# A two-layer hybrid trunk on one core: linear-attention heads with buffers of their own and half their products on GpSimd, a low-rank gate block with stacked weights, shift tiles in groups of four

## The chip, the cores and the metric

The kernel runs on one core of a Trainium2 chip. The metric is the device time of one execution in microseconds (us); a time of a kernel is the median of several runs. The profile is one further execution, recorded by the hardware profiler.

## The reference

One inference step of a two-layer trunk over 128 context tokens and 512 latent tokens (640 columns in the kernel, `T`), width 2048. Every layer is an adaptively modulated RMSNorm, one wide input projection, two mixer branches side by side, a SiLU gate path, one output projection and a gated residual. The change lies in layer 0: its modulation, and its gated linear attention (4 heads, key width 128, value width 256, forward and backward scans, decays from a projection of rank 16 per direction).

```
shift, scale, gate = split(silu(cond) @ ada_w[l] + ada_b[l], 3)       # cond: one row for context, one for latents
h = rms_norm(x, norm_g[l]) * (1 + scale) + shift

# layer 0 (even): all columns of one projection
qa, ka, va, qb, kb, vb, rb, gp = split_cols(h @ w_in, EVEN_SPLITS)    # rb: 2 * 16 columns
ya = window_sink_attention(...)  or  ctx_attention(...)
logit = einsum('btdr,drk->btdk', rb, wg) + bg                         # low-rank gate
g = log_sigmoid(logit) / 16                                           # per direction d and head
for each chunk of tokens:                                             # gla_scan, forward and backward
    bcum = cumsum(g);  qi = q*exp(bcum);  ki = k*exp(-bcum);  ks = k*exp(blast - bcum)
    o = tril(qi @ ki.T) @ v + qi @ S
    S = exp(blast) * S + ks.T @ v
yb = rms_norm(o_f + flip(o_b), gnorm)
y = concat(ya, yb) * silu(gp);   x = x + gate * (y @ w_out[0])
# layer 1 (odd): neighbourhood attention || chunked spatial gating, same frame
```

Everything is float32.

## The kernel before

**Layout.** Tokens lie along the free dimension, features along the partitions. The modulated input stands in SBUF split in two float32r halves, `acth` (rounded) and `actl` (rest), 16 k-tiles of 128 features each with 2 + 640 columns: the first two columns carry the shift of the modulation, so that each product also gives the shift's contribution. A *block* (`chunk` in the code) is 128 output columns of a weight matrix. Its weights come by DMA into `wraw`, ScalarE writes the rounded half `whi`, GpSimd the rest `wlo = wraw - whi`, four k-tiles (512 columns) at a time; `whi` and `wlo` hold 2560 columns, so five such groups. TensorE then runs three products for each k-tile and each half of the tokens: `whi*acth`, `whi*actl`, `wlo*acth`, which makes 96 matmuls of 320 or 322 columns a block (`mm_k`, recorded under line 393). All of the later blocks of the network use this scheme, many of them in pairs with one recursion of Strassen's method.

**Order.** Nothing is scheduled by the compiler. The Python code emits the instructions in one pass and keeps a model clock for each engine (`Pace`). Blocks are emitted one after the other on TensorE; between their matmuls `tick` advances generator tasks (attention heads, linear heads, normalisation) whose inputs the model holds to be ready, pumps weight splits (`wpump`) and, when VectorE is ahead, a low-priority task that computes the modulation vectors of later stages. A task that needs another's result waits for a flag (`wait`); a block's evacuation that needs one calls `need`, which lets the model clock run. So a change of one cost, buffer or flag moves many instructions around it.

**Start (`start`).** Layer 0's scale and half of its shift are computed on TensorE: 24 tiles of 128 modulation features, 1 MB each, as two loads of 512 KB into a ring of six places (`Y`, `more`). A tile takes 16 matmuls `bank<-Y,cond` with 32 output rows and 128 columns (line 1360), a copy of the result to SBUF on ScalarE (`adas<-bank`), and a product with `sel` (in the tile `small`) that puts it into two columns. The other eight shift features come from `shifts`: 32 loads of 256 KB (`raw<-ada_s`), each multiplied with a row of the condition (`crow_s`, in PSUM and in `mixrow`) on VectorE or on GpSimd and summed into `sh`. At its end `sh` goes into the first two columns of `acth` and `actl` (lines 1082 and 1083) and is transposed on TensorE (`bank<-ident,sh`). Meanwhile the first six blocks (`FIRST`, without shift columns) run in windows of k-tiles as their inputs arrive. All large loads are issued by SyncE (SP) in the order written.

**Linear heads.** The first block with shift columns is `w_rb`, the 32 low-rank columns; the kernel repeats them three times to 96 rows, since the next product wants them as hi, hi and lo. Then for each head come the blocks of k, q and two of v, and two tasks: `gla_elem` makes the decays and the products `Qp`, `KS`, `QI`, `KI` (all 128x640) for both directions, `gla_pe` does the head's matmuls, fills `O` and normalises it. One set of buffers serves all heads: `O` is `Y[:, 4:6]`, the place of `QI` and `KI`; the normalisation shares the ring `gt` with the elementwise task; there is one `k`. So the elementwise task of a head begins with

```
if h:
    yield from self.wait(f"gla_done{h - 1}")
```

and the evacuations of its k and q blocks wait for the elementwise task of the head before (`gla_elem`). After head 3 follow two gate blocks, then attention, whose heads alternate with further gate blocks.

## Time and profile before

| | before |
|---|---|
| three runs, us | 2122.69, 2121.43, 2122.52; median 2122.52 |
| the profiled execution, us | 2118.93 |
| its span, us | 2117.1 |
| mean granted TensorE clock | 0.994 |
| busy: PE, PEld | 2058.0 us (97%), 2003.7 us (95%) |
| busy: DVE, ACT, POOL | 1320.0, 1071.2, 1285.1 us (62%, 51%, 61%) |
| DMA | 341 MB, 161 GB/s on the mean; over 350 GB/s in the first two of 40 slices |

PE is TensorE's matmuls, PEld its weight loads, DVE VectorE, ACT ScalarE, POOL GpSimd, SP SyncE. A row of a list of groups reads: line, engine, operation, output<-inputs, shapes, count | busy us, mean ns of one | idle us of the engine just before these instructions, and what ended it. A float32 matmul (the 32-row ones, the products with `ones`, `sel` or a head's tiles) leaves two records, a float32r one leaves one. Line 213 is the helper through which all instructions of DVE, ACT and POOL go, line 427 that of the DMAs on SP, so groups are told apart by their tiles.

### The profile page before, as it was taken

The page shows a single profiled execution, that of the slowest core. Times are in us where ns is not written, and L with a number is a line of the kernel's source. Part 1 is how long each engine was busy: PE and PEld are TensorE (multiplying, and loading weights), DVE is VectorE, ACT ScalarE, POOL GpSimd, SP SyncE. Part 2 cuts the span into 40 slices and gives each one's busy share as a digit, 9 for nine tenths or more (in the row PEclk, how much of TensorE's full clock was granted, in tenths as well). Part 3 has the DMA queues.
Part 4 walks back from the last instruction along what each step waited for, and adds up shares of the span by engine and source line. Part 5 has one row for each costly group of instructions (what it writes and reads, how often), then busy time and mean ns, then how long its engine had stood idle before and what let it go on. Part 6 is the DMA issues. An engine that isn't in the chain of part 4 may idle for free. (4 is left out here: it accounts for less than half of the span.)

```text
span 2117.1 us, 40263 instructions
## 1 busy us (share of the span) xinstructions
PE 2058.0 (97%) x14345; PEld 2003.7 (95%) x14345; DVE 1320.0 (62%) x3063; ACT 1071.2 (51%) x2471; POOL 1285.1 (61%) x1082
## 2 busy tenths in 40 slices
PE   7999999999999999999999999999999999999996
PEld 6899999999999999999999999999999999999995
DVE  4856686666556554988666878777454444465335
ACT  5645565454666665543564444444444544454433
POOL 4756564445545544888565656655555577668873
PEclk9999999999999999999999999999999999999998
DMA  9966343336464544576643455444322344354437
GB/s 363 398 226 189 121 158 107 111 119 197 130 206 150 150 136 145 187 229 219 213 130 105 136 160 159 143 139 149 94 81 90 108 139 130 124 202 132 128 95 248
DMA packets 193401, 341.23 MB, mean 161 GB/s; under 512 B 20944, under 2 KB 70192, under 8 KB 193200
## 3 DMA queue, kind: packets, MB, share of 16 engines
q1 hardware_dynamic: 191728, 337.10, 49.4%
q8 instruction: 112, 1.84, 0.4%
q10 hardware_dynamic: 1472, 1.56, 0.2%
q14 instruction: 89, 0.73, 0.1%
HBM read 304.08 MB, written 31.88 MB: 159 GB/s over the span
## 5 line engine op out<-in xcount | busy, mean ns | idle before, releaser
L393 PE MATMUL bank<-acth,whi 128*128 128x320 f32 (+2 forms) x3320 | 1021.5, 318 | 10.6 <-ACT bc L213 2.8
L393 PE MATMUL bank<-actl,whi 128*128 128x320 f32 (+2 forms) x3320 | 994.7, 310 | 3.7 <-DMA actl<-bl_dram 2.1
L393 PE MATMUL bank<-acth,wlo 128*128 128x320 f32 (+2 forms) x3320 | 994.5, 311 | 3.5 <-POOL wlo L213 3.5
L213 POOL TENSOR_TENSOR wlo<-wraw,whi 128x512 fp32r<-128x512 f32 (+1 forms) x452 | 573.6, 1281 | 412.1 <-ACT whi L213 329.8
L393 PEld LDWEIGHTS bank<-acth,whi 128*128 128x128 f32 (+1 forms) x3320 | 617.6, 189 | 20.9 <-ACT bc L213 3.9
L393 PEld LDWEIGHTS bank<-actl,whi 128*128 128x128 f32 (+1 forms) x3320 | 617.4, 189 | 6.9 <-DMA actl<-bl_dram 3.3
L393 PEld LDWEIGHTS bank<-acth,wlo 128*128 128x128 f32 (+1 forms) x3320 | 617.5, 189 | 5.1 <-POOL wlo L213 5.1
L213 POOL TENSOR_TENSOR wlo<-rs,whi 128x384 fp32r<-128x384 f32 x370 | 408.1, 1123 | 183.2 <-ACT whi L213 143.6
L213 ACT ACTIVATE whi<-wraw 128x512 fp32r<-128x512 f32 (+1 forms) x460 | 262.9, 588 | 93.2 <-PE bank L393 60.7
L393 PE MATMUL bank<-eh,wlo 128*128 128x322 f32 (+1 forms) x666 | 207.2, 311 | 2.7 <-POOL wlo L213 2.7
L393 PE MATMUL bank<-eh,whi 128*128 128x322 f32 (+1 forms) x666 | 209.3, 314 | 0.0
L393 PE MATMUL bank<-el,whi 128*128 128x322 f32 (+1 forms) x666 | 206.9, 311 | 0.0
L213 ACT ACTIVATE whi<-rs 128x384 fp32r<-128x384 f32 x370 | 182.0, 514 | 48.5 <-PE bank L393 41.7
L213 DVE TENSOR_TENSOR wraw<-rs 128x768 f32<-128x768 f32 x74 | 98.8, 1335 | 124.7 <-POOL wlo L213 69.9
L213 DVE CUSTOM_DVE_ANT_0 adas<-adas,bank,partg 128x256 bf16<-128x256 f32 (+1 forms) x290 | 156.2, 539 | 12.6 <-DMA adas<-ada_g 5.3
L213 POOL TENSOR_TENSOR prod<-adas,mixrow 128x512 f32<-128x512 f32 x85 | 111.5, 1321 | 70.4 <-ACT prod L213 48.5
L213 ACT ACTIVATE arena<-arena,bc 128x512 f32<-128x512 f32 (+4 forms) x211 | 106.4, 527 | 79.8 <-DVE arena L213 77.0
L393 PEld LDWEIGHTS bank<-eh,wlo 128*128 128x128 f32 x666 | 125.5, 189 | 3.9 <-POOL wlo L213 3.7
L393 PEld LDWEIGHTS bank<-eh,whi 128*128 128x128 f32 x666 | 125.7, 189 | 0.1
L393 PEld LDWEIGHTS bank<-el,whi 128*128 128x128 f32 x666 | 125.8, 189 | 0.0
L213 DVE CUSTOM_DVE_ANT_0 adas<-adas,bank,part 128x512 bf16<-128x512 f32 x151 | 112.4, 744 | 9.8 <-DMA adas<-ada 6.8
L213 ACT ACTIVATE arena<-Y 128x320 f32<-128x320 f32 (+1 forms) x76 | 38.9, 512 | 152.1 <-DVE Y L213 125.9
(218 smaller groups left out, 2480.1 us busy)
## 6 DMA issues: line engine op xcount, KB each, us to landing
wraw<-w_even SPq DMA_DIRECT2D x176, 256.0 KB, 3.4
adas<-ada_g SPq DMA_DIRECT2D x128, 256.0 KB, 3.7
adas<-ada SPq DMA_DIRECT2D x128, 256.0 KB, 3.8
rs<-w_odd SPq DMA_DIRECT2D x50, 384.0 KB, 3.3
wraw<-w_odd SPq DMA_DIRECT2D x74, 256.0 KB, 3.5
wraw<-w_out SPq DMA_DIRECT2D x64, 256.0 KB, 3.9
rs<-w_odd SPq DMA_DIRECT2D x50, 256.0 KB, 3.8
Y<-ada SPq DMA_DIRECT2D x24, 512.0 KB, 7.3
```

Source lines behind the costliest of these rows:

```text
L213: return f(*args, **kw)
L393: self.nc.tensor.matmul(out, lhsT, rhs, start=start, stop=stop, **kw)
```

## The change

1. **Low-rank block.** The weights keep 32 columns; `whi` now holds hi and lo side by side (64 columns), and two products per k-tile and half, with `acth` and with `actl`, make 64 matmuls with 64 output rows (`quad`). Both token halves are copied to SBUF, and a float32 product with a 0/1 matrix `rep` adds hi and lo rows and repeats the sum to 96 rows.
2. **Start.** The eight shift tiles go in two groups of four: 16 matmuls of 512 columns, loads waited for and refilled four at a time, one copy of 512 columns, four products with `sel`. The copy of the very first tile moves from ACT to DVE. `cT` is loaded by ACT's queue instead of SP's; the constants needed later (`late`, 176 KB, and the sinks) are loaded after the start. `mixrow` has one place instead of two.
3. **Linear heads.** `O` of heads 0 to 2 lies in `YB`, the normalisation has a ring `nt` of its own, `k` has two places, `Qp` and `QI` are made on GpSimd. The elementwise task waits for the one before it; `gla_free` of the head before (its last read of `Qp`) is awaited ahead of the first `Qp`, and its `gla_done` ahead of writing `O`. Gate block 14, which lies in the place of `O`, needs `gla_done2`.
4. **Attention.** Gate block 2 moves from before head 7's query block to behind it.

```
+GROUPS = (*((f, 1) for f in range(KT)), *((f, 4) for f in range(KT, KT + BOTH, 4)))
...
-        nc.sync.dma_start(self.cT, d["cT"])
+        nc.scalar.dma_start(self.cT, d["cT"])
...
-        self.mixrow = [self.t(yb, [128, PIECE], "mixrow", bufs=2) for _ in range(2)]
+        self.mixrow = [self.t(yb, [128, PIECE], "mixrow")] * 2
...
-        if m < M:
-            raw = raw[:, :, None, :].to_broadcast([128, n, M // m, m])
-            hi, lo = (x.rearrange("p a (b c) -> p a b c", c=m) for x in hl)
+        if key[0] in self.stacked:
+            hl = hi
+            hi, lo = hl[:, :, :m], hl[:, :, m:]
         nc.scalar.activation(hi, raw, AF.Copy)
...
+    def quad(self, c, parts):
...
+        for half, p in enumerate(banks):
+            cs = self.cols(half, shift)
+            n = cs.stop - cs.start
+            for u in units:
+                w = self.wget(u)
+                for j in range(4):
+                    for i, x in enumerate((self.ah, self.al)):
+                        k = u[1] + j
+                        self.mm(p[:M, :n], w[:, j, :], x[:, k, cs], start=k == i == 0, stop=k == KT - 1 and i == 1)
+                    if j % 2:
+                        self.tick()
+            self.nc.scalar.activation(parts[half][:M, :n], p[:M, :n], AF.Copy)
+            self.drop(p)
+        for u in units:
+            self.wdone(u)
+
+        def work():
+            for half, x in enumerate(parts):
...
+                yield from self.until(x)
+                yield from self.bank()
+                p = self.sm()
+                self.mm(p[:96, : x.shape[1]], self.rep[:M, :], x)
+                evac(*((None, p) if half else (p, None)))
+                yield
...
             def tiles():
-                for i in range(KT + BOTH):
-                    ws = [ring[(2 * i + q) % NR].rearrange("p (a b) -> p a b", b=128) for q in range(2)]
-                    yield from self.until(*ws)
...
+                for i, n in GROUPS:
+                    m = 8 // n
+                    for b in range(0, 2 * n, 4):
+                        e = min(b + 4, 2 * n)
+                        ws = [ring[(at + q) % NR].rearrange("p (a b) -> p a b", b=128 * n) for q in range(e - b)]
+                        yield from self.until(*ws)
+                        self.now += 0.2
+                        for k in range(m * b, m * e):
+                            g = 32 * (k % 4)
+                            o, c, w = pm[g : g + 32, 0 : 128 * n], cond[:, k, :], ws[k // m - b][:, k % m, :]
+                            self.pe(0.0575 * n, o, c, w)
+                            nc.tensor.matmul(o, c, w, start=k < 4, stop=k >= KT - 4)
...
+                        for q in range(e - b):
+                            load(at + q + NR)
...
+                    r = rows.next()[:, : 128 * n]
+                    if i == 0:
+                        nc.vector.tensor_copy(r, pm[:, : 128 * n])
+                    else:
+                        nc.scalar.activation(r, pm[:, : 128 * n], AF.Copy)
...
+            nc.sync.dma_start(self.late, d["late"])
+            nc.sync.dma_start(self.sink, d["attn_sink"].partition_broadcast(128))
             while self.tasks or self.low:
...
         if h:
-            yield from self.wait(f"gla_done{h - 1}")
+            yield from self.wait(f"gla_elem{h - 1}")
...
-            nc.vector.tensor_tensor(L["Qp"][dr], q, e3, ALU.mult)
+            if dr and h:
+                yield from self.wait(f"gla_free{h - 1}")
+            nc.gpsimd.tensor_tensor(L["Qp"][dr], q, e3, ALU.mult)
...
-            nc.vector.tensor_tensor(L["QI"][dr], q, e4, ALU.mult)
+            nc.gpsimd.tensor_tensor(L["QI"][dr], q, e4, ALU.mult)
...
+        if h:
+            yield from self.wait(f"gla_done{h - 1}")
         yield from self.until(At, Sb)
         outs((0, 1), (None, S))
...
-        sq, sq2 = L["gt"].next(), L["gt"].next()
+        sq, sq2 = L["nt"].next(), L["nt"].next()
...
+                self.need("gla_done2")
                 ev(pa, pb)
...
-            L["O"] = Y[:, 4:6, :]
+            L["O"] = (*(self.YB[:, KT - NY - 2 :, :],) * 3, Y[:, 4:6, :])
...
-            add(wE[16 + h], 128, True, None, lazy("k", pre=p))
+            add(wE[16 + h], 128, True, None, lazy("k", pre=(f"gla_elem{h - 2}",) if h > 1 else (), then=keep))
...
-                if kv and h != 5:
+                if h in (4, 6):
...
-        for i in (3, 4, 5):
+        for i in (2, 3, 4, 5):
             gate_chunk(wE[28 + i], self.yt(i), (f"ya{i}",), "gx")
```

TensorE at the end of the low-rank block, before: the last two k-tiles of `w_rb` in bank 68, then the first k-tile of head 0's keys in bank 69.

```order
L393 MATMUL bank_68<-acth,whi 96x320
L393 MATMUL bank_68<-actl,whi 96x320
L393 MATMUL bank_68<-acth,wlo 96x320
L393 MATMUL bank_69<-acth,whi 128x322
L393 MATMUL bank_69<-actl,whi 128x322
L393 MATMUL bank_69<-acth,wlo 128x322
```

The same place in the change; `late` is the tile that holds `rep`, `arena` the copy of the block's result.

```order
L398 MATMUL bank_68<-acth,whi 64x320
L398 MATMUL bank_68<-actl,whi 64x320
L398 MATMUL bank_69<-acth,whi 128x322
L398 MATMUL bank_69<-actl,whi 128x322
L398 MATMUL bank_69<-acth,wlo 128x322
L398 MATMUL bank_69<-acth,whi 128x322
L398 MATMUL bank_69<-actl,whi 128x322
L398 MATMUL bank_69<-acth,wlo 128x322
L398 MATMUL bank_71<-arena_1538,late 96x322
```

The third product of each k-tile is gone (32 of 96 matmuls), and two float32 products with `rep` stand between the matmuls of the next block, one for each half of the tokens.

SP at the end of the modulation tiles, before: the last two tile loads (`more<-ada ... x2`) and what stands ahead of them.

```order
L427 DMA raw_303<-ada_s 128x512
L427 DMA raw_304<-ada_s 128x512
L427 DMA Y<-ada 128x1024 x2
L427 DMA raw_305<-ada_s 128x512
L427 DMA raw_306<-ada_s 128x512
L427 DMA wraw<-w_even 128x512
L427 DMA Y<-ada 128x1024
L427 DMA more_127<-ada 128x1024
L427 DMA wraw<-w_even 128x512
L427 DMA more_127<-ada 128x1024 x2
L427 DMA raw_302<-crow_s 128x512
L427 DMA raw_303<-crow_s 128x512
```

The same in the change, up to its last two tile loads.

```order
L432 DMA more_127<-ada 128x1024 x3
L432 DMA raw_301<-crow_s 128x512
L432 DMA raw_302<-crow_s 128x512
L432 DMA wraw<-w_even 128x512
L432 DMA Y<-ada 128x1024 x3
L432 DMA more_127<-ada 128x1024
L432 DMA raw_303<-ada_s 128x512
L432 DMA wraw<-w_even 128x512
L432 DMA raw_304<-ada_s 128x512
L432 DMA raw_305<-ada_s 128x512
L432 DMA raw_301<-ada_s 128x512
L432 DMA more_127<-ada 128x1024 x2
```

The two `crow_s` rows that open the third quarter of the shift work, and four more of its pieces, now stand ahead of the last two tile loads: up to and with these SP has issued 20 pieces and 6 `crow_s` rows, against 16 and 4 before. On TensorE the count of block matmuls behind the last tile falls from 198 to 174, and the transposition of `sh` stands 48 block matmuls ahead of `w_rb` instead of 18.

GpSimd during head 0's elementwise work in the change; `Y<-arena` are the products `Qp` and `QI`. Before there is only `wlo`, `prod` and the gates' `YB` here.

```order
L214 TENSOR_TENSOR wlo<-wraw,whi 128x512 x4
L214 TENSOR_TENSOR Y<-arena_1538 128x640
L214 TENSOR_TENSOR wlo<-wraw,whi 128x512
L214 TENSOR_TENSOR Y<-arena_1538 128x640
L214 TENSOR_TENSOR wlo<-wraw,whi 128x512 x3
L214 TENSOR_TENSOR Y<-arena_1538 128x640 x2
L214 TENSOR_TENSOR wlo<-wraw,whi 128x512 x2
```

Four products of 128x640 for each head stand between the weight splits on GpSimd's queue, 16 in all; as many are gone from VectorE's.

113 lines of the change are left out of this document (65 added, 48 removed).

## The prediction

> **What bounds the kernel now.** I read the page's first part, then a table of stages, then what TensorE waited for. Columns of the table: stretch, its length, then PE, PEld, DVE, ACT and POOL busy, granted clock, DMA share, GB/s.
>
> ```profile
> span 2117.1 us, 40263 instructions
> PE 2058.0 (97%) x14345; PEld 2003.7 (95%) x14345; DVE 1320.0 (62%) x3063; ACT 1071.2 (51%) x2471; POOL 1285.1 (61%) x1082
> 0.00:144.36 144.36, 128.71 (x1397) 115.53 (x1398) 90.95 (x192) 76.66 (x173) 85.97 (x77) 0.99 0.91 338
> 144.36:560.00 415.64, 407.94 (x2788) 400.00 (x2787) 275.23 (x543) 226.46 (x483) 224.01 (x162) 1.00 0.47 146
> 560.00:1110.00 550.00, 536.22 (x3552) 520.44 (x3551) 361.35 (x874) 312.35 (x749) 338.06 (x280) 1.00 0.55 175
> 1110.00:2117.10 1007.10, 985.13 (x6613) 967.71 (x6611) 592.45 (x1457) 455.76 (x1066) 637.05 (x565) 0.99 0.43 135
> 10.00:110.00 100.00, 94.11 (x1123) 82.83 (x1124) 67.69 (x125) 58.91 (x133) 63.17 (x45) 0.98 1.02 394
> ```
>
> TensorE has work for 97% of the span. Its idle time is 15.7 us in the start (144.36 less 128.71), 7.7 us in the low-rank block and the linear heads (144 to 560), 13.8 us in attention and the first projection, 22.0 us after. So two things can move the time: TensorE's own work, and these 59 us. In the start a second limit lies close: between 10 and 110 us the DMA engines are full (1.02) at 394 GB/s while TensorE is busy 94 of 100 us.
>
> What TensorE waited for between 144 and 560 us (total, times, longest), and its wait for weight splits in the whole run:
>
> ```profile
> PE bank L393 <- ACT bc L213: 2.9, 3, 1.6
> PE bank L398 <- ACT arena L213: 2.5, 5, 0.9
> PE bank L393 <- DVE arena L213: 1.4, 4, 0.4
> PE bank L398 <- DVE Y L213: 0.5, 1, 0.5
> PE bank L393 <- POOL wlo L213: 6.2, 8, 1.4
> ```
>
> There is no long wait at a head's boundary: the heads are already covered by blocks, and no split came late among them (the last row's eight waits lie elsewhere).
>
> **Term 1, the low-rank block.** It runs without a gap, and the products with `ones` price the two new float32 products:
>
> ```profile
> 144.36:158.48 14.12, 14.12 (x98) 14.12 (x97) 5.54 (x15) 6.50 (x15) 9.16 (x9) 1.00 0.76 239
> L393 PE MATMUL bank<-arena,ones 128*128 128x320 f32 x28 | 9.1, 435 | 0.7 <-ACT arena L213 0.7
> ```
>
> 14.12 us for 96 matmuls are 0.147 us each, so 32 fewer save 4.7 us. Fourteen products with `ones` (two records each) took 9.1 us, 0.65 each with their ends; the two with `rep` cost 1.3 at that price, and half of it if their tails overlap the next block. I take 1.2: **-3.5 us**, bounds -4.1 and -3.4. The copies of the block and the added step delay the 96-row gate by some 2 us; it is first needed by head 0's elementwise task, which also waits for k and q, two blocks of 14 us, and these hide it.
>
> **Term 2, the start.** TensorE's work there hardly changes. One tile's 16 matmuls take 1.08 us; a group's 16 of 512 columns, shared by four groups of array columns, take 4.1 if I go by a plain 512-column float32 product (eight in 8.2 us), against 4.3 for four tiles.
>
> ```profile
> L393 PE MATMUL bank<-arena 128*128 128x512 f32 x16 | 8.2, 595 | 0.0
> 108.01 0.65 PE L1360 MATMUL bank<-Y,cond 128*32 128x128 f32 x16
> 111.48 1.40 PE L1360 MATMUL bank<-more,cond 128*32 128x128 f32 x32
> 116.64 0.38 PE L393 MATMUL bank<-small,adas 128*128 128x2 f32 x2 [1.81 <-ACT adas L213]
> 141.61 0.27 PE L398 MATMUL bank<-ident,sh 128*32 128x128 f32 x1
> 144.36 0.31 PE L393 MATMUL bank<-acth,whi 128*96 128x322 f32 x1
> 0.74 0.39 SPq L279 DMA_DIRECT2D cT<-cT  x1
> 1.18 0.90 SPq L427 DMA_DIRECT2D Y<-ada  x2
> ```
>
> The order of the DMAs does change. SP lands its loads one after the other, and in the change four more pieces and two more rows of 256 KB, 1.57 MB, stand ahead of the last two tile loads. At 394 GB/s that is 4.0 us; the loads start 0.44 us earlier, since `cT` leaves the queue (0.74 to 1.18). Before, the last tile ran at 111.48, 1.40 us instead of 1.08, so it already waited a little for its data. I put the end of the last group at 112.9 + 3.5 = 116.4. Behind it stand 174 block matmuls instead of 198: 25.6 us at 0.147, four products with `sel` and the transposition 1.1 + 0.3, and some wait for the copy (1.81 before; six matmuls cover part): 144.0 against 144.36. **-0.4 us.** Were TensorE not held by the loads, its earlier first tile and fewer waits would give -2.5; a full 1.8 us wait at the `sel` products gives +1.
>
> The shift work must end before the transposition, now 30 matmuls (4.4 us) earlier in TensorE's order, at about 136.7:
>
> ```profile
> 115.42 0.75 DVE L213 CUSTOM_DVE_ANT_0 adas<-raw,bank,sh 128x512 bf16<-128x512 f32 x1 [4.60 <-DMA raw<-ada_s]
> 138.96 0.91 DVE L213 TENSOR_TENSOR sh<-sh,psum 128x8 f32<-128x8 f32 x4
> 140.37 0.19 DVE L1083 TENSOR_TENSOR actl<-sh,acth 128x32 fp32r<-128x32 f32 x1 [0.30 <-ACT acth L1082]
> ```
>
> Before, the last two quarters (16 pieces) ran from 115.42 to 140.56, 25.1 us. In the change the third quarter's first piece stands 2.4 MB, 6 us, ahead of the last tile load, so it lands near 109.5, and the work would end near 134.6. That is 2 us to spare; it costs nothing if it holds.
>
> **Term 3, the linear heads.** The heads' matmuls are the same. Of the 7.7 us of idle time, 1.6 (at 176.14) is an evacuation held up in ACT's queue, which the change does not touch; the waits of transposes and state products on their own copies (ACT arena, DVE arena, 3.9 in all) are chains inside one head. What separate buffers can take away are the other waits for evacuations and for `Y`, about 1.8 us, and some of the short ones. **-2 us**, bounds -6 and, by the rival below, far above zero. The moved products:
>
> ```profile
> L213 DVE TENSOR_TENSOR Y<-arena 128x640 f32<-128x640 f32 x24 | 26.1, 1099 | 4.9 <-ACT arena L213 4.8
> L213 POOL TENSOR_TENSOR actl<-Y,acth 128x640 fp32r<-128x640 f32 x14 | 21.3, 1529 | 8.6 <-ACT acth L213 8.6
> L213 POOL TENSOR_TENSOR YB<-YB,Y 128x640 f32<-128x640 f32 x7 | 12.6, 1804 | 8.4 <-DVE Y L213 8.4
> 276.22 1.92 DVE L213 TENSOR_TENSOR Y<-arena 128x640 f32<-128x640 f32 x1
> 280.69 0.81 DVE L213 TENSOR_TENSOR arena<-arena 128x640 f32<-128x640 f32 x1
> 273.14 6.14 POOL L213 TENSOR_TENSOR wlo<-wraw,whi 128x512 fp32r<-128x512 f32 x3
> L213 POOL TENSOR_TENSOR wlo<-wraw,whi 128x512 fp32r<-128x512 f32 x300 | 406.2, 1360 | 325.1 <-ACT whi L213 254.8 <-issue 21.2 <-PE bank L393 16.4
> ```
>
> VectorE loses 16 products of 1.10 us, 18 us; GpSimd gains 16 of about 1.6 (between 1.53 and 1.80), 26 us, on 224 busy of 416. Nothing is hidden in VectorE's gain: TensorE waited for it 1.9 us here. Product and split share something: a VectorE product took 1.92 us while GpSimd ran three splits (273.14 to 279.28), and 0.81 just after. The Trainium skill, "SBUF — State Buffer", section "Who interferes with whom", calls this an exclusive lock: a VectorE instruction with two SBUF inputs and a GpSimd one that reads SBUF shut each other out for the whole instruction. The trace agrees (1.92 against 0.81). By that rule at its worst, VectorE stands still for all 26 us of new GpSimd work and gains nothing, so that term 3 would be 0 and the sum 2118.5.
>
> **Edits at nothing.** The two late loads (180 KB) go where the DMA share is under 0.8. With one `mixrow` a GpSimd product waits at a quarter's change, and nobody on TensorE waits for that. Gate block 2 behind head 7 is the same work in another place. `need("gla_done2")` holds back an evacuation four blocks, 57 us, after head 2's matmuls; if it came late, TensorE's next blocks would queue behind it. From 560 us on I take nothing, within 2 us either way, since the recording order shifts there too.
>
> **The sum.** -3.5 - 0.4 - 2 = -5.9 us. On the profiled execution that is 2118.93 to 2113.0. That execution lies 3.6 us under the median of the runs, 2122.52; the runs would come to 2116.6. A measurement can tell about 0.2%, 4.2 us, from no change: faster is under 2118.3, slower over 2126.7.
>
> **The rivals.** *The shift work does not move up* (chance 0.17): its pieces queue on VectorE behind the tiles' work and end at 140.1 as before. Then the transposition stands from 136.7 to 140.3, and everything after it 3.6 us later: 2120.2, within 0.2%. For it: between 10 and 110 us VectorE was already 68% busy. Against it: the third quarter's data comes 6 us ahead.
>
> *GpSimd's queue becomes the bound in the heads* (0.18). A product waits at the head of the queue for its exponential and for the last reader of `Qp`; the next `wlo` stands behind it, and TensorE behind that. A block needs a split every 3.5 us, a split takes 1.36, so 2.2 us are spare, enough for one product of 1.6, not for two in a row or one that waits. It decides once GpSimd is late by more than the groups split ahead (up to three, 10 us). If each of the eight direction passes costs one wait of 1.4, the longest in the trace, that is +11 in place of term 3's -2: 2129.6, slower. The Trainium skill, "GPSIMD Engine Reference", section "Engine selection", advises against two-input elementwise work there, about twice as slow as on VectorE; the rows give 1.6 against 1.10 or 0.81 alone. Against this rival: not one late split among the heads before, at 54% busy.
>
> *More comes out* (0.10): the tails of the `rep` products hide (-4.1), the start gives -2.5, the heads -6: 2109.9.
>
> **How the numbers follow.** My forecast holds 0.55, 2111 to 2120 by the bounds of its terms; a tenth of that lies above 2118.3. Faster: 0.52 + 0.10 = 0.62. Within 0.2%: 0.03 + 0.17 = 0.20. Slower: 0.18. For the range I go from 2110, below which half of the last rival lies, to 2128, which takes in the shift rival and the milder part of the GpSimd one; some 0.19 is left out.
>
> **What would show it.** Right: the low-rank block about 9.4 us long with two `rep` products after it; the last tile group ending at 115 to 117 and the block beginning near 144; TensorE's idle time between there and the end of head 3 near 6 us; the same waits as before from 1110 on. Wrong: a wait of TensorE on `sh` at the transposition (shift rival), waits `PE <- POOL wlo` between the heads' blocks (GpSimd rival), a wait on `ada` tiles of more than 2 us, or a sum of idle time after 560 that differs by more than 2 us.

## The result, and the profile after

| | median, us | runs |
|---|---|---|
| before | 2121.17 (2118.11 to 2125.98) | 18 |
| the change | 2126.1 (2119.8 to 2130.41) | 18 |

The ratio is 1.0024, 95% interval 1.0016 to 1.0032: the change is slower by about 5 us, where 5.9 us of gain were forecast. The interval lies wholly above 1. The profiled execution took 2125.59 us (before 2118.93).

From the page of the change its span and busy times, then its table of stages; the cuts lie at the same points of TensorE's work as in the table of before (start of the low-rank block, then of attention, then of layer 1's long run of blocks), and the last row is the stretch in which loads fill the DMA engines.

```profile
span 2123.8 us, 39788 instructions
PE 2060.8 (97%) x14125; PEld 2000.4 (94%) x14125; DVE 1310.3 (62%) x3067; ACT 1064.9 (50%) x2447; POOL 1302.9 (61%) x1090
...
0.00:151.35 151.35, 132.94 (x1205) 113.62 (x1206) 86.65 (x199) 73.50 (x161) 80.26 (x75) 0.97 0.90 325
151.35:571.50 420.15, 409.12 (x2762) 400.00 (x2761) 278.60 (x539) 221.15 (x466) 235.43 (x170) 0.99 0.45 143
571.50:1120.70 549.20, 536.10 (x3551) 520.91 (x3550) 352.36 (x874) 313.88 (x754) 346.10 (x283) 0.99 0.55 176
1120.70:2123.80 1003.10, 982.65 (x6613) 965.85 (x6611) 592.72 (x1457) 456.33 (x1066) 641.14 (x565) 0.99 0.43 135
...
10.00:110.00 100.00, 90.48 (x903) 76.74 (x904) 61.79 (x127) 54.34 (x118) 56.35 (x41) 0.95 1.00 366
```

The start is 7.0 us longer (151.35 against 144.36). The second stage is 4.5 us longer although it holds less work: its idle time is 11.0 us (420.15 less 409.12), before 7.7. TensorE's busy time there did not fall either (409.1 against 407.9), because its clock was lower (0.99 against 1.00). In the last row the DMA engines moved 366 GB/s, before 394.

I also put both traces side by side at the same matmul of TensorE's order. The change loses 7.1 us up to the low-rank block; wins 1.1 through the block and the first keys (before's 143.9 to 193.7 us), and 4.1 through the heads (to 484); loses 7.0 in the opening of attention (to 651), 2.2 more by 1054 and 0.2 by 1847; and gets 4.6 back after that. The sum is +6.7. So there are two places to explain, the start and the opening of attention, and one to check, the block, whose 3.5 us nearly vanished.

**The start.** TensorE in the change: the last tile group, the products with `sel`, the transposition of `sh`, the low-rank block's first matmul.

```profile
121.80 1.68 PE L1404 MATMUL bank<-more,cond 128*32 128x512 f32 x10
125.73 1.05 PE L398 MATMUL bank<-small,adas 128*128 128x2 f32 x8 [1.18 <-ACT adas L214]
144.33 0.27 PE L403 MATMUL bank<-ident,sh 128*32 128x128 f32 x1
151.49 0.31 PE L398 MATMUL bank<-acth,whi 128*64 128x322 f32 x1
```

The group ends at 123.5 instead of the forecast 116.4, and all behind it is late by about that. `sh` is not what TensorE waits for: there is no idle time ahead of the transposition, though `sh` was ready only 0.1 us before it (its last step on VectorE ends at 144.2). What SP's queue waited for between 10 and 115 us, of before and of the change (total, times, longest; line 1360 or 1404 are the tiles' matmuls, which free the ring's places):

```profile
SPq L427 <- PE bank L1360: 6.4, 5, 2.7
```

```profile
SPq L432 <- PE bank L1404: 11.8, 9, 3.5
```

SP issues in order. A refill whose place TensorE has not yet freed holds up every load behind it, and these waits are twice as long.

**The block.** In the change: TensorE's two products with `rep`, then ScalarE and GpSimd around the second one, and the clock after it (columns of the stage table).

```profile
161.83 0.78 PE L398 MATMUL bank<-arena,late 64*96 64x322 f32 x2
166.15 0.78 PE L398 MATMUL bank<-arena,late 64*96 64x320 f32 x2 [2.45 <-ACT arena L214]
...
163.83 0.63 ACT L214 ACTIVATE prod<-prod 128x512 f32<-128x512 f32 x1 [1.40 <-POOL prod L214]
165.06 0.63 ACT L214 ACTIVATE prod<-prod 128x512 f32<-128x512 f32 x1 [0.50 <-POOL prod L214]
165.69 0.41 ACT L214 ACTIVATE arena<-bank 64x320 f32<-64x320 f32 x1
...
162.51 3.73 POOL L214 TENSOR_TENSOR prod<-adas,mixrow 128x512 f32<-128x512 f32 x3 [8.45 <-ACT mixrow L214]
...
166.15:170.50 4.35, 4.35 (x16) 3.88 (x17) 2.30 (x7) 4.04 (x11) 3.69 (x4) 0.62 0.60 186
```

The copy of the block's second half stands in ScalarE's queue behind sums of the low-priority modulation, which wait for GpSimd's products. TensorE waits 2.45 us for it, and then runs 14 of the next block's matmuls at 0.263 us instead of 0.147, 1.6 us more. With these and the two products the block's saving is more than used up: at before's 170 us the change is 8.2 us late, 1.1 more than at the block's start. What the stage wins comes behind that, 1.7 us of it at a wait of before (1.56 us at 176.14) that does not occur in the change.

**The opening of attention.** In the change, TensorE's waits there, VectorE and ScalarE ahead of them, and the clock after:

```profile
521.43 0.33 PE L403 MATMUL bank<-ident,arena 128*128 128x128 f32 x1 [2.60 <-ACT arena L214]
523.12 1.12 PE L403 MATMUL bank<-ident,arena 128*128 128x128 f32 x4 [1.36 <-ACT arena L214]
...
519.58 0.75 DVE L214 CUSTOM_DVE_ANT_0 adas<-adas,bank,partg 128x512 bf16<-128x512 f32 x1 [0.32 <-DMA adas<-ada_g]
520.25 0.49 DVE L214 TENSOR_TENSOR arena<-bank,rstd 128x320 f32<-128x320 f32 x1
521.15 0.75 DVE L214 CUSTOM_DVE_ANT_0 adas<-adas,bank,partg 128x512 bf16<-128x512 f32 x1 [0.41 <-DMA adas<-ada_g]
...
520.78 0.17 ACT L214 ACTIVATE bc<-bank 128x2 f32<-128x2 f32 x1 [2.18 <-DVE arena L214]
...
524.30:529.10 4.80, 4.80 (x20) 4.80 (x20) 4.39 (x13) 2.40 (x7) 3.65 (x3) 0.51 0.58 177
```

It is much the same pattern on VectorE: the evacuations of a head's block (`arena<-bank,rstd`) stand behind and between modulation pieces of 0.75 us each, some of which wait 0.3 to 0.4 us for their data, and TensorE's transposes (`ident,arena`) wait for them. The mixture alone is not what is new. Before's VectorE has it too, but its first evacuation runs 16 block matmuls ahead of the transposes; in the change no block matmul lies between the two. The same pair in before, VectorE and TensorE:

```profile
513.72 0.49 DVE L213 TENSOR_TENSOR arena<-bank,rstd 128x320 f32<-128x320 f32 x1
...
516.15 0.27 PE L398 MATMUL bank<-ident,arena 128*128 128x128 f32 x1
```

The wait again costs clock, 18 matmuls at 0.264, 2.1 us. Over this stretch TensorE idles 6.3 us, before 2.2.

### The profile page after: what moved, and what is told of

The parts are those of the page before. It is cut to its first block, busy times and chain, and to the rows that moved or that the text cites. A ratio compares the mean times of both kernels' runs of the same rounds, so it can differ in the third digit from the quotient of the medians.

```text
span 2123.8 us, 39788 instructions
## 1 busy us (share of the span) xinstructions
PE 2060.8 (97%) x14125; PEld 2000.4 (94%) x14125; DVE 1310.3 (62%) x3067; ACT 1064.9 (50%) x2447; POOL 1302.9 (61%) x1090
## 5 line engine op out<-in xcount | busy, mean ns | idle before, releaser
L398 PE MATMUL bank<-acth,wlo 128*128 128x320 f32 (+1 forms) x3288 | 986.2, 311 | 2.1 <-POOL wlo L214 2.1
L398 PEld LDWEIGHTS bank<-acth,wlo 128*128 128x128 f32 x3288 | 614.7, 190 | 2.9 <-POOL wlo L214 2.9
L214 DVE CUSTOM_DVE_ANT_0 adas<-adas,bank,partg 128x256 bf16<-128x256 f32 (+1 forms) x297 | 161.3, 543 | 15.6 <-DMA adas<-ada_g 8.1
L214 POOL TENSOR_TENSOR prod<-adas,mixrow 128x512 f32<-128x512 f32 x80 | 104.5, 1317 | 51.9 <-ACT prod L214 31.1
L214 POOL TENSOR_TENSOR arena<-arena 128x320 f32<-128x320 f32 (+1 forms) x66 | 70.6, 1069 | 68.2 <-ACT arena L214 60.1
```

The source lines that it names most:

```text
L214: return f(*args, **kw)
L398: self.nc.tensor.matmul(out, lhsT, rhs, start=start, stop=stop, **kw)
```

## Experiments

Three groups: which part of the change costs the time (1 to 4), what the order in which the code emits its instructions costs by itself (5 to 8), and each part by itself (9 to 18). Ratios are against the kernel before in runs of the same chip, whose median lay between 2119.2 and 2121.4.

### 1 to 4: the parts alone

**after_ones**, the change with single tiles. My first theory was that the groups of four hold back the loads.

```
-GROUPS = (*((f, 1) for f in range(KT)), *((f, 4) for f in range(KT, KT + BOTH, 4)))
+GROUPS = tuple((f, 1) for f in range(KT + BOTH))
```

> The changed kernel with the eight shift tiles one at a time again (GROUPS holds 24 single tiles; all else as in the change). Theory A, the start: in the change the last tile load landed at 122.4 us instead of 112.2, and TensorE reached the low-rank block 7.0 us later; taken alone that is the loss. Then the block begins at 144 to 146 here and the time is 5 to 7 us under the changed kernel's, near 2120. Theory B, the heads and what follows: TensorE lost 7.2 us between 500 and 620 us (it was 2.0 us later than before at 485 us and 9.2 us later at 710), by the overlap of the heads itself; then an earlier start is lost again there and the time stays within 2 us of the changed kernel's.

2130.38 us, ratio 1.0043 [1.0031, 1.0054]; the block began 9.0 us later than before. Single tiles make it worse, so that theory falls; theory B, within 2 us of the change, fails as well.

**quad_only**, part 1 of the change alone; **start_only**, part 2 alone; **heads_only**, part 3 (with one `mixrow`, as its buffers need).

```
quad_only:  before + two products per k-tile, copies and `rep` for the low-rank block
start_only: before + groups of four, copy of the first tile on DVE, `cT` on ACT's queue
heads_only: before + own O, nt ring, two k, Qp and QI on GpSimd, their waits
```

> The kernel before with the low-rank block in 64 matmuls and two rep products, alone. The block takes 9.4 us by either theory. In the changed kernel the second rep product then waited 2.45 us for ScalarE's copy, which stood in ScalarE's queue behind accumulations of the modulation task that waited for GpSimd's products, and the next 14 matmuls ran at 0.26 us each instead of 0.147 (1.6 us more). If that wait belongs to the block (theory A), the gain is gone here too: 0 to +1 us against the kernel before. If it comes from the later start of the changed kernel only, the gain of 3.5 us shows: 3 to 4 us faster.

> The kernel before with the edits of the start alone: shift tiles in two groups of four, cT on ScalarE's queue, the first tile's copy on VectorE, late constants, one mixrow; the low-rank block and the heads as before. Theory A: the low-rank block begins at 150 to 152 us instead of 144.4 and the time is 6 to 7 us above the kernel before. Theory B: what the start loses is won back by later waits that fall away, and the time is within 2 us of the kernel before.

> The kernel before with the edits of the linear heads alone: O and norm buffers of their own, two key buffers, Qp and QI on GpSimd, gla_done2 for gate block 14; one mixrow, which these buffers need room for. Theory A: the heads gain some 4 to 6 us up to the end of head 3 (in the changed kernel the lag fell from 8.2 us at 170 us to 2.0 at 485), and the time is 3 to 6 us under the kernel before. Theory B: the loss between 500 and 620 us shows here as well, 5 to 7 us, and the time is equal to the kernel before's or up to 3 us above it.

| | median, us | ratio [95%] | start | block to 194 us | heads | opening of attention |
|---|---|---|---|---|---|---|
| quad_only | 2123.11 | 1.0015 [1.0007, 1.0024] | +4.1 | -3.6 | +5.1 | -1.3 |
| start_only | 2123.14 | 1.0021 [1.0011, 1.0031] | +2.5 | +1.1 | +0.5 | -0.4 |
| heads_only | 2129.03 | 1.0034 [1.0022, 1.0046] | -0.3 | -0.4 | +1.4 | +8.1 |
| the change | 2126.1 | 1.0024 [1.0016, 1.0032] | +7.1 | -1.1 | -4.1 | +7.0 |

(The stages are those of the profiled execution, less before's. That of quad_only was the slowest of its 12 runs, 2129.04, so its row is rough.) None of the three parts gains, and none lies in a range that was expected of it. Their losses do not add up either: 3.3 + 3.4 + 9.3 us against 4.9 together. In quad_only the block's saving is there (-3.6), but its start, whose instructions are before's up to 130 us, came out 4 us late, and a new wait among the heads cost more:

```profile
384.68 0.48 PE L399 MATMUL bank<-ident,Y 128*128 128x128 f32 x1 [5.01 <-DVE Y L213]
```

This is what made me suspect the order: an edit of a block at 150 us changes what VectorE does first at 380.

### 5 to 8: the order alone

TensorE's work stays exactly the same and one constant of the model clock, by which the code decides what to emit next, is made 5 ns larger from the end of the start on: the cost of a VectorE, GpSimd or ScalarE instruction.

```
before_nv, after_nv: +self.pace.COST = {**Pace.COST, "v": (0.075, 1 / 960)}     # 0.070
before_ng:           the same for GpSimd, 0.040 to 0.045
after_na:            +self.pace.COST = {**Pace.COST, "a": (0.1, 0.84 / 1000)}   # 0.095
```

> The kernel before; one constant of its model clock (the fixed cost of a VectorE instruction, 70 ns) is set to 75 ns after the start. No instruction is added or taken away; from head 0's normalisation on the emitted order differs from the kernel before's. Theory C, the order: what the three parts of the change lose lies mostly in stretches that they do not touch, since each moves the order in which the modulation task's pieces and the heads' steps meet, and the order of the kernel before happens to be a good one: 4 to 10 us slower than the kernel before, with waits of 2 us or more on VectorE or ScalarE between 480 and 900 us. Theory B, the edits of the heads themselves cost the time: within 2 us of the kernel before.

> The same with the model's fixed cost of a GpSimd instruction (40 ns set to 45 ns after the start). Theory C: 4 to 10 us slower than the kernel before, the waits in other places than with the constant of VectorE. Theory B: within 2 us of the kernel before.

> The changed kernel with the same 5 ns on VectorE's constant. Theory C: it moves by several us either way against the changed kernel's 2126.1, since that one is a draw among orders too: 2120 to 2132. Theory B: 2126 within 2 us.

> The changed kernel with the model's fixed cost of a ScalarE instruction at 100 ns in place of 95 after the start. Theory C: 2120 to 2132, another value than with VectorE's constant. Theory B: 2126 within 2 us.

| | median, us | ratio to before [95%] |
|---|---|---|
| before_nv | 2134.99 | 1.0058 [1.004, 1.0075] |
| before_ng | 2131.26 | 1.0043 [1.003, 1.0055] |
| after_nv | 2133.2 | 1.0052 [1.0037, 1.0067] |
| after_na | 2139.13 | 1.0081 [1.0066, 1.0096] |

Four of four reorderings cost time with no matmul added: 10 and 14 us on the kernel before by the medians, and by the ratios 6 and 12 us on the change (1.0052 and 1.0081 against 1.0024). Three of the four lie above what theory C expected. Both kernels' own orders are better than these draws, and a change of the work by 6 us is lost in what another order may cost. Two limits: all four runs raise a constant and none lowers one, and the model clock also picks the engine of some copies, so the order is not all that moves (in before_nv VectorE has 14 instructions fewer and ScalarE 14 more). What such an order costs is seen in after_na at head 3's end, TensorE, then ScalarE and VectorE:

```profile
495.54 0.64 PE L398 MATMUL bank<-acth,whi 128*128 128x320 f32 x1 [6.12 <-ACT bc L214]
...
495.32 0.17 ACT L214 ACTIVATE bc<-bank 128x2 f32<-128x2 f32 x1 [4.87 <-DVE arena L214]
...
490.48 0.82 DVE L214 SCALAR_TENSOR_TENSOR arena<-arena 128x640 f32<-128x640 f32 x1 [4.08 <-ACT arena L214]
```

A gate block cannot be evacuated because VectorE stands for 4.1 us at the head of its queue on one instruction of the normalisation, with the evacuation behind it.

### 9, 10, 13 and 16: parts in the order of before

In these kernels the order is held: the model clock is charged with the old work, so that everything but the named instructions is emitted exactly as in before. What they show is the edit, not the order.

**quad_frozen**: only the low-rank block is new, its `rep` products 8 to 12 matmuls behind its copies on ScalarE.

```
+for i, b in enumerate((self.ah, self.al)):
+    self.nc.tensor.matmul(p[:64, :n], hi[:, 0:64], b[:, k, cs], ...)
...
+self.nc.scalar.eng.activation(x, q[:64, :n], AF.Copy)
+self.backlog.append([2, issue])        # issue: the product with rep
```

> The kernel before with the low-rank block in 64 matmuls, and everything else held in the order of the kernel before: the model clock is charged with the old 96 matmuls, so only the block's own instructions differ; each half's rep product stands 8 to 12 matmuls behind its copy on ScalarE. If the block's price of the prediction is right and only the order of the rest spoilt it (theory C): 3 to 4 us faster than the kernel before, and no new wait of over 1 us from 160 us on. Rival: the time saved is waited for again soon after (data or another engine sets the pace), then within 1 us of the kernel before.

2122.79 us, ratio 1.0016 [1.0007, 1.0024]. The block itself takes 9.4 us (146.96 to 156.33) instead of 14.1, 4.7 us shorter, as forecast. Then, TensorE and ScalarE of this kernel:

```profile
160.78 1.39 PE L812 MATMUL bank<-arena,late 64*96 64x322 f32 x2 [4.29 <-ACT arena L809]
...
158.46 0.63 ACT L217 ACTIVATE prod<-prod 128x512 f32<-128x512 f32 x1 [1.73 <-POOL prod L217]
...
159.68 0.63 ACT L217 ACTIVATE prod<-prod 128x512 f32<-128x512 f32 x1 [0.50 <-POOL prod L217]
...
160.31 0.42 ACT L809 ACTIVATE arena<-bank 64x322 f32<-64x322 f32 x1
```

All of the saving goes into one wait for the copy, 4.29 us, 1.2 us of slow clock behind it, and the two products themselves.

**quad_late** gives the `rep` products banks of their own and puts them about 10 us later.

```
+self.nc.tensor.matmul(o[:96, :n], self.rep[0:64, :], x, ...)   # o = self.banks[3 + half]
-self.backlog.append([2, issue])
+self.backlog.append([12 - 2 * half, issue])
```

> As quad_frozen (the kernel before in its own order, low-rank block in 64 matmuls), but the two rep products and what follows them stand some 10 us behind the block, so that TensorE does not wait for ScalarE's copy, which stood 4.3 us behind accumulations of the modulation task there. If that wait is all that ate the block's saving (theory D, a queue with a waiting instruction at its head): the block's 32 matmuls (4.4 us) less the two products (1.3 to 1.5 us), 3 us faster than the kernel before from 170 us on, and 2 to 4 us in the median. Rival: the time is waited for again further on; within 1 us.

2120.19 us, ratio 1.0004 [0.9995, 1.0013]. TensorE no longer waits at `rep`, but at the next block's second bank, for the same copy, which frees it:

```profile
159.06 0.41 PE L410 MATMUL bank<-acth,whi 128*128 128x320 f32 x1 [2.62 <-ACT arena L820]
...
167.85 1.32 PE L823 MATMUL bank<-arena,late 64*96 64x322 f32 x4
```

**quad_hold** puts the modulation's instructions that fall into the block's second half behind the block's copies.

```
+if self.chunks[c][1] == 96 and k == 8:
+    self.lowheld = []          # the low-priority task's instructions go here
...
+for f in self.lowheld: f()     # and out again, behind the copies
```

> As quad_late (the kernel before in its own order, low-rank block in 64 matmuls, rep products a few microseconds behind it), but what the modulation task issues during the second half of the block stands behind the block's two copies on ScalarE, VectorE and GpSimd, not ahead of them; nothing else moves. If the queue ahead of the copies was all that ate the saving (theory D): no wait at 155 to 162 us, the next block 3 to 4 us earlier than in the kernel before, and 2 to 4 us less in the median. Rival: the modulation's pieces, now 3 to 5 us later, hold up the evacuation of head 0's blocks at 175 us, and the time stays within 1 us of the kernel before.

2122.11 us, ratio 1.0007 [0.9998, 1.0016]. The cause of the wait at the copy is shown by this: there is none from 155 to 162 us, and the next block begins 4.7 us earlier against the start. Then TensorE waits at 178, and ScalarE shows for what; the last row is the same place in before:

```profile
177.94 0.64 PE L411 MATMUL bank<-acth,whi 128*128 128x320 f32 x1 [5.23 <-ACT bc L228]
...
177.20 0.60 ACT L228 ACTIVATE bank<-adas 128x512 f32<-128x512 f32 x1 [4.12 <-DMA adas<-shift_s]
177.74 0.15 ACT L228 ACTIVATE bc<-bank 128x2 f32<-128x2 f32 x1
```

```profile
175.40 0.60 ACT L213 ACTIVATE bank<-adas 128x512 f32<-128x512 f32 x1 [2.20 <-DMA adas<-shift_s]
```

A piece of the modulation stands on ScalarE, waiting 4.12 us for its load, ahead of the small copy (`bc`) that an evacuation needs. It is not one of the pieces held back (those are issued from line 224) and not new: in before it waits 2.20 us for the same load, and TensorE 1.56 us behind it. It runs 31.0 us after the block's start in before and 31.4 here. So the load came no earlier for the shorter block, and the saved time is waited for one block later.

**pool_frozen**: only the engine of the 16 products `Qp` and `QI` is changed.

```
-nc.vector.tensor_tensor(L["Qp"][dr], q, e3, ALU.mult)
+nc.gpsimd.eng.tensor_tensor(L["Qp"][dr], q, e3, ALU.mult)      # likewise QI
```

> The kernel before, its order held in the same way; only the 16 products Qp and QI of the linear heads are issued by GpSimd instead of VectorE, at the same places. Theory C: the move by itself does next to nothing, -2 to +1 us. The rival of the prediction, GpSimd's queue as the bound in the heads: waits of TensorE for wlo among the heads and +5 to +11 us.

2122.09 us, ratio 1.0016 [1.0006, 1.0027]. That is slower than before, beyond the +1 of theory C. TensorE waited for no weight split among the heads, so the GpSimd rival's mechanism is absent. VectorE's two-input products fell from 72.6 to 65.2 us, by 7.4 where 18 were moved. The loss of 4.1 us lies in one place. The product there in before, and then VectorE, GpSimd and TensorE of this kernel:

```profile
203.09 0.81 DVE L213 TENSOR_TENSOR arena<-arena 128x640 f32<-128x640 f32 x1
```

```profile
203.03 1.91 DVE L217 TENSOR_TENSOR arena<-arena 128x640 f32<-128x640 f32 x1
...
200.27 2.16 POOL L1740 TENSOR_TENSOR Y<-arena 128x640 f32<-128x640 f32 x1
202.41 1.84 POOL L217 TENSOR_TENSOR wlo<-wraw,whi 128x512 fp32r<-128x512 f32 x1
...
206.59 0.41 PE L397 MATMUL bank<-acth,whi 128*128 128x320 f32 x1 [1.61 <-ACT bc L217]
209.23 0.90 PE L402 MATMUL bank<-ident,arena 128*128 128x128 f32 x3 [1.39 <-ACT arena L217]
```

GpSimd ran a moved product and a split back to back, VectorE's product took 1.91 us beside them, and TensorE waited twice for what stands behind it. Its granted clock was 0.74 from 204 to 217 us.

### 11, 12, 14, 15, 17 and 18: the start

**start_pieces**: start_only, the third quarter of the shift work loaded only after all tiles.

```
+if i >= third and "loads" not in self.flags:
+    held.append(i)
```

> The start's edits alone (as start_only), but the third quarter of the shift work may load only once all tile loads are issued, so 16 pieces and 4 rows stand ahead of the last tile load again instead of 20 and 6. If those 1.57 MB make the start late: the last tile load lands near 114 us instead of 117.8, and the time is 2 to 4 us under start_only's, unless TensorE then waits for sh at the transposition, which would give the 2 to 4 us back. If the groups of four make it late: no change against start_only.

2123.28 us, ratio 1.0014 [1.0004, 1.0024]. The last tile load landed at 117.0 instead of 117.8, the transposition of `sh` moved to 145.9, close ahead of the block, and the block began 3.4 us late (start_only 2.5). No gain.

**start_ones**: start_only with single tiles (the edit of after_ones).

> The start's edits alone (as start_only), with the eight shift tiles one at a time again. If the groups of four make the start late: the kernel before's time within 1.5 us. If the order of the loads does: as start_only or later, the last tile load near 118 to 122 us.

2129.77 us, ratio 1.0045 [1.0029, 1.0062]; the block began 8.7 us late. The groups of four are worth 5 us by the ratios (6.6 by the medians) within the changed start.

**start_sq**: start_only, the square of an x tile on ScalarE put behind the copy of the same modulation tile, because on ScalarE in the change such a square, waiting for its load, stood ahead of a copy that TensorE waited 1.93 us for (the two rows). **start_ones_sq**: the same with single tiles. **best**: start_sq together with quad_late's block.

```profile
87.46 0.74 ACT L214 ACTIVATE adas<-Y 128x640 f32<-128x640 f32 x1 [3.39 <-DMA Y<-xT]
88.10 0.26 ACT L214 ACTIVATE adas<-bank 128x128 f32<-128x128 f32 x1
```

```
+if f > 1:
+    yield from self.wait(f"copy{f}")     # ahead of the square of tile f
```

> The start's edits alone (as start_only), with one rule more: on ScalarE the square of x tile f stands behind the copy of modulation tile f, as it always does in the kernel before; with the change's own order five squares stand ahead, and one of them waits 3 to 4 us for its load while TensorE waits for the copy behind it. Theory D: the waits of 1.5 to 2.5 us for that copy at 86 to 88 us are gone, tile loads 29 to 33 land 2 to 4 us earlier, and the time falls by 2 to 4 us against start_only's 2123.1, to the kernel before's or under it. Rival: the load is late for another reason and the wait moves to the load itself: no change.

> start_sq and quad_late together, heads and order as in the kernel before. Theory D: the sum of both, 2 to 6 us faster than the kernel before. Rival: no faster than the kernel before.

> start_ones (the start's edits with single tiles, 2129.8 us) with the rule of start_sq: on ScalarE the square of x tile f stands behind the copy of modulation tile f. If that order is what makes the start late (theory D): the 2.5 us wait at 87 us is gone, the last tile load lands near 115 us instead of 122, and the time is 5 to 9 us under start_ones's. Rival: another of the start's edits does it, and the time stays within 2 us of start_ones's.

start_sq 2120.9 us, 1.0005 [0.9996, 1.0015]: the wait is gone, and it is the only changed start that a measurement cannot tell from before. What was expected of its start did not come, though: in its profile the last tile load landed at 120.2 (start_only 117.8) and the block began 4.3 us late. best 2122.59, 1.0013 [1.0003, 1.0024], not the 2 to 6 us of gain expected. start_ones_sq 2128.11, 1.0043 [1.0029, 1.0056], no better than start_ones. The squares are not the main cause.

**start_order**: start_only, the shift work's loads held to their places of before.

```
+AHEAD = (14, 14, 14, 14, 20, 20, ...)      # tile loads ahead of each piece in before
+while held and self.sent >= AHEAD[held[0]]:
+    self.dma(...)
```

> The start's edits alone (low-rank gate in one block, fours), with the shift work's loads held to the places among the tile loads that they have in the kernel before; the products and the heads are as before. In the changed starts 30.2 MB stand in program order ahead of the 34th tile load, where the kernel before has 28.7 MB: 1.5 MB, 3.8 us at the start's 394 GB/s. If the order of the loads is what the start lost: the 34th tile load lands near 84 to 86 us instead of 88 to 93, the last near 112 to 115 instead of 117.8, the block begins 1 to 4 us earlier than with the start's edits alone, and the time is 2118 to 2121, at the kernel before's or under it. If another edit of the start is the cause: the time of the start's edits alone, 2123.1, within 1 us, or the tile of shifted rows becomes what the block waits for and the block begins no earlier.

2124.35 us, ratio 1.0017 [1.0008, 1.0026]. The 34th tile load landed at 86.8 us, but the last at 117.4, as in start_only, though as many bytes are issued up to it as in before (41.7 MB by the sizes on the page; in start_only and the change 43.3). The block began 4.9 us late, since 18 more of its neighbours' matmuls stand behind the last tile. So neither start_order nor start_pieces won back the 4 us counted for the bytes put ahead. Their supplies, 376 and 372 GB/s, were also lower than start_only's 384, so single profiles do not give the order of the loads a price of its own; by the medians it was worth nothing. Of three kernels, what SP waited for (10 to 115 us) and the load stretch; start_order, start_only, and heads_only, whose start is before's:

```profile
SPq L432 <- PE bank L1373: 15.8, 12, 4.4
...
10.00:110.00 100.00, 90.41 (x916) 75.28 (x916) 58.99 (x120) 53.51 (x116) 56.07 (x40) 0.97 1.00 376
```

```profile
SPq L431 <- PE bank L1368: 10.0, 9, 3.8
...
10.00:110.00 100.00, 89.11 (x933) 74.12 (x926) 63.19 (x127) 55.68 (x121) 57.77 (x41) 1.00 1.02 384
```

```profile
SPq L427 <- PE bank L1360: 6.6, 5, 2.8
...
10.00:110.00 100.00, 93.09 (x1122) 81.61 (x1123) 68.39 (x125) 59.06 (x133) 63.46 (x45) 0.98 1.02 393
```

The last column closes the account, as bookkeeping. Against before's 394 GB/s, start_only moved 1.0 MB less in these 100 us, which is 2.5 us of loading; the change (366) 2.8 MB less, 7.1 us. The forecast end of the last group, 116.4, counted 4.0 us for the bytes put ahead and nothing for the supply. With 2.5 and 7.1 us more it is 118.9 and 123.5, which is where the two kernels end it. (start_order: 1.8 MB less, 4.6 us, and no bytes ahead give 117.1; it ended at 118.5.) Over all profiles, eleven of changed starts ran at 364 to 386 GB/s, 376 on the mean, and nine of before's start at 379 to 395, 388 on the mean.

Why the supply is lower is not settled. SP's waits for ring places were 6.9 to 15.8 us in the changed starts and 3.9 to 8.6 in before's, which points to TensorE coming later to its tiles; but among profiles of one start the supply does not follow them (quad_only: 5.0 us at 379 GB/s), and no run took these waits away alone. Nor does the share column show the DMA engines idle instead: it is 1.02 in before and in start_only, at 394 and 384 GB/s, and 1.00 in the change, at 366. The share fell by 2% where the rate fell by 7%.

## Why the prediction was wrong

Its time, 2116.6, was too low by 9.5 us and its sign was wrong. 2126.1 lies inside its range only because that takes in the rivals.

**Term 2, the start, failed.** -0.4 was forecast, with +1 as the bad end; in three profiles with the change's start (the change, after_nv, after_na) the block began 6.0 to 7.9 us late, in nine with before's start 1.3 us on the mean. The 4.0 us for the bytes put ahead fit the account, but no run shows them by themselves. The shift work ended at 144.2 and not 134.6, but the tiles had made all else as late, and the transposition at 144.33 did not wait. The step that failed is "at 394 GB/s": I took the supply of before's profile as given because the DMA engines were full, where the change runs at 366; why it does stays open. The sign named in advance, the last group ending at 115 to 117, said so at once.

**Term 1, the block, was right in its work and wrong in its cover.** 4.7 us of matmuls saved (quad_frozen) and two `rep` products after it, as forecast. The step that failed is that the copies' delay is hidden by the two blocks ahead of the first use. I asked who needs the 96 rows, and not what stands ahead of the copies on ScalarE, nor who stands behind the `rep` product on TensorE. That product waits 2.45 us and everything behind it with it. quad_late and quad_hold show that it is no matter of place: the bank, or the next evacuation behind a load that comes no earlier, takes over the wait.

**Term 3, the heads, was right in size and not by its reason.** -4.1 in the heads of the change lies in the bounds (-6 to far above zero), but heads_only gave +1.4 in the same stretch. Counted in block matmuls, head 2's elementwise work begins 72 earlier than before, head 1's 12 later and head 3's at the same one, so the buffers of their own moved one head forward and not the end of the stage. Which edit gave the -4.1 is not shown. A product took 1.79 us on GpSimd (the group in the change, below), the upper end of the estimate; in pool_frozen VectorE got back 7.4 of 18 us. The Trainium skill's rule that was weighed against the term ("SBUF — State Buffer", "Who interferes with whom": the two engines shut each other out) was nearer than the plain sum: 1.91 us against 0.81 beside GpSimd's work, and six tenths of the gain gone.

```profile
L214 POOL TENSOR_TENSOR Y<-arena 128x640 f32<-128x640 f32 x16 | 28.6, 1791 | 0.0
```

**"From 560 us on nothing, within 2 us either way" failed.** From 484 us on the change loses 4.7 us, 7.0 of it in the opening of attention. The four profiled kernels beside it that hold the heads' edits lose 7 to 12 us there; of those without them, the two reorderings lose 4 to 5, start_only and quad_only nothing, and quad_frozen 2.8. That it is the evacuations queued behind modulation pieces is read from one trace; which of the heads' edits brings that order about was not separated.

**The rivals.** The shift work was not waited for in the change, if only by 0.1 us, and no weight split was late among the heads. The GpSimd rival's time (2129.6) came nearer than the forecast, but by another mechanism. What was missing is the rival that happened: that another order of instructions is worth some 10 us against a gain of 6. How much of the change's own loss is order was not measured: no run holds the whole change, or its heads' buffers, in the order of before. Two small slips of the prediction change nothing: term 3 at 0 gives 2118.6, not 2118.5, and a tenth of 0.55 is 0.055, not 0.03.

No version beat the kernel before. quad_late and start_sq equal it within the measurement.

## What to carry to other kernels

In a program whose order comes out of a cost model, change one constant of that model by a few per cent first: if the time moves by more than an edit is to gain, only an order that is held can show what the edit does. Before a delay is called hidden, ask of each in-order queue what stands ahead of the new instruction and what stands behind the one that waits for it; a saving that leaves the same copy behind the same queue comes back as a wait at the next bank or evacuation. A full DMA share in one profile is not a supply that a changed order will have too.

## What the runs showed of the hardware

A wait of TensorE of 2.45 us was followed by a granted clock of 0.50 from 167.2 to 170.6 us in the change, 3.4 us long; at two waits close together, 2.60 and 1.36 us, it was 0.50 from 522.1 to 529.0, 6.8 us long. The matmuls took 0.263 us instead of 0.147 there, so the two drops cost 1.6 and 2.1 us on top of the waits. Not every such wait is followed by a drop: behind this one of start_only the granted clock was 1.00.

```profile
180.00 0.41 PE L397 MATMUL bank<-acth,whi 128*128 128x320 f32 x1 [2.90 <-ACT bc L214]
```

The Trainium skill, "TensorE: Matmul & The Clock Gate", section "Part 1: The HAM clock gate (the "warmup" mystery)", puts the drop behind an idle window of about 3.4 us and the recovery behind a busy one as long. The 3.4 us of the first recovery agree and the second took twice that, while the drops came after shorter waits here.

A stage that lives on the DMA engines scatters by itself. Before's start, the same instructions up to 130 us in nine profiled executions, was supplied at 379 to 395 GB/s, and its end follows: the low-rank block began 4.1 us later than in before's profile at 379 (quad_only), 2.6 and 1.9 at 384, 0.8 at 390, and 0.4 earlier at 395 (pool_frozen); 10 GB/s are 2.5 us. Before's own profile, at 394, is one of the fast ones, and the prediction was made against it. The load stretch of quad_only:

```profile
10.00:110.00 100.00, 91.31 (x1074) 80.25 (x1075) 66.15 (x122) 58.60 (x131) 61.79 (x45) 0.98 1.01 379
```
